# A two-layer attention encoder: rows of the input in natural order, swapped queries from DRAM, and the order of mask steps

## The chip, the core and the metric

The kernel runs on one core of one Trainium2 chip. The metric is the device time of one execution in microseconds (us). [...] VectorE is DVE, ScalarE is ACT, GpSimd is POOL; SyncE (SP) issues all DMAs.

## What is computed

Two sequences, a prompt of 1024 tokens and a sample of 512, each get 16 meta tokens in front and pass through two layers. Cut to what matters:

```
def layer(x):                                   # x: (1040 or 528) x 1024
    h = rmsnorm(x, pre_g)                       # x * rsqrt(mean(x*x) + 1e-6) * pre_g
    aq, ak, av, ag, bq, bk, bv, bg = split(h @ w_in)
    oa = window_gqa_attention(rope(aq), rope(ak), av, sink) * silu(ag)
    ob = diff_attention(rope(bq), rope(bk), bv, lam) * silu(bg)
    return x + rmsnorm(concat(oa, ob) @ w_out, post_g)
```

The windowed part has 8 query heads of 64 in 2 groups; each query sees the 16 meta tokens, the keys at a distance of at most 128, and a sink logit. The other part has 4 heads of the difference of two softmaxes over all keys. All is 32-bit.

## The kernel before, in words

**Tiling.** The 1040 + 528 = 1568 tokens lie side by side as columns, in four chunks of 392 (`CH`, L30). In layer 0 the chunks hold the tokens `ICH[0]` (L32-35): 0 to 391, 392 to 783, then 256 + 120 = 376 of them from two places, then 392. Features lie on partitions, eight blocks of 128. Each large product is made as three products of f32r halves (hi x hi, hi x lo, lo x hi), so every operand of PE is a pair of tiles.

**Order.** Every operation is first recorded with a priority; `schedule()` (L329-445) then plays a model of the engines, of the DMAs and of the buffers of each pool, and writes out one fixed order for each engine, which `emit()` (L447) issues. All instructions therefore carry line L451, and are told apart by their tiles. An engine works off its order strictly. Buffers of a pool come round in the order in which they are taken: `slot` has 16, `pp` 4 (raw weights, and much else later), `ps_t` 2 and `ps_s` 1 (both PSUM, `ps_s` of three banks), `qq` 2 (queries), `st` 1 (staged values on their way to DRAM). `START` (L50) ranks the first loads: weight 0, chunk 0, chunk 1, weight 1, the rotary table, weight 2, chunk 2, chunk 3, weight 3.

**The start of layer 0.** `load_x` (L608) brings each chunk from `xT`, the transposed input, so with features on 128 partitions: four loads for chunk 0, two for each other chunk (four for chunk 2, whose tokens come from two places). Chunk 0 is split into halves at once (L1499-1510), its scale by 1/rms is put on later. For chunks 1 to 3 `start_stats` (L1496) calls `prestats` (L723): squares on ACT or POOL, sums over the eight feature blocks on DVE, then `rstd_bc` (L693) sums over partitions with four transposes on PE, a reduce on DVE and a power on POOL, and spreads the result over all partitions with four more transposes on PE. `prenorm` (L751) then multiplies each of the eight blocks by that and by the gain, copies the high half and subtracts for the low half. The products of the first unit's four weights with the four chunks follow (`inproj`).

**The start of layer 1** is another: `pre` (L1464) takes rows that lie in natural order with tokens on partitions, already scaled, transposes four tiles of a feature block into one `ps_t` buffer, and evicts them twice: a copy with the gain (high half), and gain times value minus the high half on DVE. `stat` (L1402) makes the scale of a row: two squarings on ACT that sum along the row, one small step on DVE and one on POOL.

**Units.** Each layer then has six units: four heads of difference attention (`attn_b`) and two groups of windowed attention (`attn_a`, L1065), each overlapped with the next unit's products (`inproj`) or, at the end, with `outproj`. `attn_a` goes over the two sequences and their tiles of 128 queries, 4 heads a tile; the heads are taken in batches of three that share one `ps_s` buffer (L1145). For each tile the queries come from `AQ` in DRAM into `qt[:, 0]`; two copies from SBUF to SBUF fill `qt[:, 1]` with the two halves of the partitions swapped (L1155-1165). The three scores of a batch are followed by their mask steps, a custom instruction on DVE that adds the mask and takes the extreme of the row. One line makes the order's model hold each mask step back until the last of the three scores:

```
nc.extra = [nc.last]                       # L1176, behind the three scores
for bi, (u, i) in enumerate(batch):
```

Of the kernel before, what the change touches and what calls it, by code (L numbers as in the profile page):

```python
# [26 lines left out]
EPS = 1e-6  # L27
# [25 lines left out]
QUICK = 1  # L53
# [5 lines left out]
PRE_ACT = (0, 0, 0, 0, 0, 0, 0, 0)  # L59
# [4 lines left out]
ONLY = 4  # L64
# [478 lines left out]
def hymba_kernel(ctx, tc, xT, xr, w_in, w_out, rope, masks, pre_g, post_g, sub_g, sink_b, sink_m, lam_in, yo):  # L543
# [56 lines left out]
    def f32(ap):  # L600
        return ap.bitcast(F32)
# [6 lines left out]
    def load_x(ci):  # L608
        xin[ci] = pair()
        nc.boost = START[f"x{ci}"] * 100000  # L610
        w = 2 if ci == 0 else 4
        for k in range(0, 8, w):
            o = 0
            for t0, m in ICH[0][ci]:
                dma(xin[ci][k // 4][:, k % 4:k % 4 + w, o:o + m],
                    xT.rearrange("(a p) t -> p a t", p=128)[:, k:k + w, t0:t0 + m])
                o += m
        nc.boost = 0
# [104 lines left out]
    def prestats(xs, tmp, n, only=False):  # L723
        if only:
            for i in range(4):
                r = slice(2 * (i % 2), 2 * (i % 2) + 2)
                x, y = xs[i // 2][:, r, 0:n], tmp[i // 2][:, r, 0:n]
                nc.any((nc.scalar, "activation", (y, x, AF.Square), {}),
                       (nc.gpsimd, "tensor_tensor", (y, x, x), dict(op=ALU.mult)))
                if i:  # L730
                    nc.vector.tensor_tensor(
                        tmp[0][:, 0:2, 0:n], tmp[0][:, 0:2, 0:n], tmp[i // 2][:, r, 0:n], op=ALU.add)
            nc.vector.tensor_tensor(tmp[0][:, 0, 0:n], tmp[0][:, 0, 0:n], tmp[0][:, 1, 0:n], op=ALU.add)
        else:
            for i in range(2):
                nc.scalar.activation(tmp[i][:, :, 0:n], xs[i][:, :, 0:n], AF.Square)
            nc.any_tt(tmp[0][:, :, 0:n], tmp[0][:, :, 0:n], tmp[1][:, :, 0:n], ALU.add)
            for k in (2, 1):
                nc.any_tt(tmp[0][:, 0:k, 0:n], tmp[0][:, 0:k, 0:n], tmp[0][:, k:2 * k, 0:n], ALU.add)
        return rstd_bc(tmp[0][:, 0, 0:n], n, 1.0 / D)  # L740

    def scaled(out, x, g, rb, n, act):
        for j in range(x.shape[1]):
            if act:
                nc.scalar.activation(out[:, j, 0:n], x[:, j, 0:n], AF.Copy, scale=g[:, j:j + 1])
                nc.any_tt(out[:, j, 0:n], out[:, j, 0:n], rb[:, 0:n], ALU.mult)
            else:
                nc.vector.scalar_tensor_tensor(
                    out[:, j, 0:n], x[:, j, 0:n], g[:, j:j + 1], rb[:, 0:n], op0=ALU.mult, op1=ALU.mult)

    def prenorm(l, ci, xs, rb, n):  # L751
        his, los = [], []
        for i in range(2):
            hi, lo = pair(F32R)
            for j in range(4):
                r = slice(j, j + 1)
                h = at_p([128, 1, CN])
                scaled(h, xs[i][:, r], preg[:, l, 4 * i + j:4 * i + j + 1], rb, n, PRE_ACT[2 * ci + i])
                h = h[:, :, 0:n]
                nc.any_copy(hi[:, r, 0:n], h)  # L760
                if l == 0 and ci < QUICK:
                    nc.vector.tensor_tensor(lo[:, r, 0:n], h, f32(hi[:, r, 0:n]), op=ALU.subtract)
                else:
                    nc.any_tt(lo[:, r, 0:n], h, f32(hi[:, r, 0:n]), ALU.subtract)
            his.append(hi)
            los.append(lo)
        hT[ci] = (rows(his, 4), rows(los, 4))
# [324 lines left out]
    def attn_a(l, g):  # L1092
        S = SC[l]
        AK, AV, AQ = S["AK"][g], S["AV"][g], S["AQ"][g]
        for s in range(2):
# [502 lines left out]
```

## Time and profile before

| | |
|---|---|
| median of 3 runs | 1938.57 us (1936.39 to 1941.69) |
| the profiled execution | 1938.61 us |
| its span in the profile | 1936.8 us |
| mean granted clock of TensorE | 0.985 |
| busy: PE, DVE, ACT, POOL | 1843.4, 1515.2, 1008.1, 279.3 us |
| DMA traffic | 273.02 MB, 141 GB/s in the mean |

The span runs from the first to the last instruction of the profiled execution. Busy times are sums over instructions; an engine that is not busy stands still because something it needs is late, or because it has nothing to do. The views below give this for a stretch of the span, for a group of instructions of one form, or for single instructions in order of time.

### The profile page before, as it was taken

The page shows a single profiled execution, that of the slowest core. Times are in us where ns is not written, and L with a number is a line of the kernel's source. Part 1 is how long each engine was busy: PE and PEld are TensorE (multiplying, and loading weights), DVE is VectorE, ACT ScalarE, POOL GpSimd, SP SyncE. Part 2 cuts the span into 40 slices and gives each one's busy share as a digit, 9 for nine tenths or more (in the row PEclk, how much of TensorE's full clock was granted, in tenths as well). Part 3 has the DMA queues.
Part 4 walks back from the last instruction along what each step waited for, and adds up shares of the span by engine and source line. Part 5 has one row for each costly group of instructions (what it writes and reads, how often), then busy time and mean ns, then how long its engine had stood idle before and what let it go on. Part 6 is the DMA issues. An engine that isn't in the chain of part 4 may idle for free.

```text
span 1936.8 us, 35552 instructions
## 1 busy us (share of the span) xinstructions
PE 1843.4 (95%) x12328; PEld 1771.3 (91%) x12328; DVE 1515.2 (78%) x3363; ACT 1008.1 (52%) x2417; POOL 279.3 (14%) x516
## 2 busy tenths in 40 slices
PE   6999999999999989999789999999999999999998
PEld 5989989999989889999789999999999999889998
DVE  8858788888787787587988397787967859869767
ACT  4335445454444475575765254454545438648632
POOL 3001111211121210000221021121111101101001
PEclk8999999999999999999989999999999999999999
DMA  7253363544543657556354535445353475684464
GB/s 252 56 161 105 110 170 102 148 119 109 153 117 108 154 144 198 118 133 178 120 196 116 152 100 160 120 118 161 98 167 114 124 180 125 159 229 99 109 205 150
DMA packets 299147, 273.02 MB, mean 141 GB/s; under 512 B 101560, under 2 KB 263480, under 8 KB 298840
## 3 DMA queue, kind: packets, MB, share of 16 engines
q1 hardware_dynamic: 298968, 270.75, 50.5%
q8 instruction: 98, 1.61, 0.4%
q14 instruction: 81, 0.66, 0.1%
HBM read 149.19 MB, written 96.01 MB: 127 GB/s over the span
## 4 chain that ended last, share of the span: by engine, by line
PE 70%; DVE 11%; DMA 8%; ACT 4%; issue 4%; SPq 2%; POOL 1%; DVEq 0%; POOLq 0%; ACTq 0%
PE ps_d L451 43%; PE ps_s L451 10%; PE ps_o L451 9%; PE ps_t L451 8%; DVE at L451 2%; DVE pp L451 2%; DVE slot L451 2%; ACT pp L451 2%; SPq L451 2%; DVE sm L451 1%; DMA vv<-BV 1%; DVE og L451 1%; DMA kk<-AK 1%; DVE ru L451 1%; POOL sm L451 1%
## 5 line engine op out<-in xcount | busy, mean ns | idle before, releaser
L451 PE MATMUL ps_d<-slot,whl 128*128 128x392 f32 (+2 forms) x4560 | 938.2, 347 | 15.0 <-ACT slot L451 6.7
L451 PEld LDWEIGHTS ps_d<-slot,whl 128*128 128x128 f32 x4560 | 785.7, 190 | 22.2 <-ACT slot L451 6.7
L451 PE MATMUL ps_s<-kk,qq 128*128 128x264 f32 (+9 forms) x1496 | 284.4, 319 | 21.7 <-ACT pp L451 5.7
L451 PE MATMUL ps_o<-at,vv 128*128 128x256 f32 (+6 forms) x1368 | 285.9, 307 | 8.4 <-DVE og L451 5.5
L451 ACT ACTIVATE at<-ps_t 128x256 fp32r<-128x256 f32 (+9 forms) x434 | 187.7, 439 | 202.7 <-PE ps_t L451 177.4
L451 ACT ACTIVATE pp<-ps_s,sm 116x1040 f32<-116x1040 f32 (+4 forms) x208 | 203.9, 980 | 169.9 <-DVE sm L451 161.5
L451 DVE TENSOR_TENSOR at<-ps_t,at 128x256 fp32r<-128x256 f32 (+6 forms) x472 | 224.5, 480 | 68.0 <-ACT at L451 53.5
L451 PEld LDWEIGHTS ps_s<-kk,qq 128*128 128x128 f32 (+4 forms) x1496 | 227.2, 185 | 46.9 <-ACT pp L451 9.0
L451 PE MATMUL ps_d<-whl,slot 128*128 128x256 f32 x1800 | 259.0, 288 | 8.6 <-DVE slot L451 6.0
L451 PEld LDWEIGHTS ps_d<-whl,slot 128*128 128x128 f32 x1800 | 235.1, 192 | 14.3 <-DVE slot L451 7.2
L451 DVE TENSOR_REDUCE sm<-ps_s 116x1 f32<-116x1040 f32 (+4 forms) x208 | 218.3, 1050 | 34.3 <-PE ps_s L451 33.3
L451 ACT ACTIVATE pp<-pp,sm 128x336 f32<-128x336 f32 (+6 forms) x347 | 206.6, 607 | 61.0 <-DVE sm L451 57.6
L451 PEld LDWEIGHTS ps_o<-at,vv 128*128 128x128 f32 (+1 forms) x1368 | 214.0, 190 | 16.8 <-ACT pp L451 5.4
L451 PE MATMUL ps_t<-ident,pp 128*128 128x128 f32 (+6 forms) x1248 | 203.5, 269 | 3.1 <-DVE at L451 1.6
L451 POOL TENSOR_TENSOR pad<-pp,pad 128x64 fp32r<-128x64 f32 (+3 forms) x145 | 53.2, 370 | 819.0 <-ACT pad L451 528.1
L451 PEld LDWEIGHTS ps_t<-ident,pp 128*128 128x128 f32 (+6 forms) x1248 | 147.8, 137 | 14.7 <-ACT pp L451 2.8
L451 DVE CUSTOM_DVE_ANT_0 pp<-ps_s,mk,nsinks 128x336 f32<-128x336 f32 (+2 forms) x192 | 97.1, 528 | 22.1 <-PE ps_s L451 20.3
L451 POOL TENSOR_TENSOR sm<-sm 128x2 f32<-128x2 f32 (+3 forms) x112 | 48.7, 437 | 408.2 <-DVE sm L451 404.6
L451 POOL TENSOR_TENSOR sm<-sm,mhalf 128x1 f32<-128x1 f32 (+7 forms) x98 | 80.8, 830 | 132.9 <-DVE sm L451 129.6
L451 ACT ACTIVATE og<-ps_o 64x128 f32<-64x128 f32 (+4 forms) x248 | 66.1, 287 | 44.8 <-PE ps_o L451 27.3
L451 ACT ACTIVATE ru<-ps_d 128x392 f32<-128x392 f32 (+5 forms) x100 | 48.7, 487 | 73.9 <-PE ps_d L451 64.2
L451 DVE TENSOR_TENSOR slot<-slot 128x512 f32<-128x512 f32 (+3 forms) x79 | 73.9, 945 | 8.4 <-ACT slot L451 8.0
(158 smaller groups left out, 2130.3 us busy)
## 6 DMA issues: line engine op xcount, KB each, us to landing
wraw<-in_w_in_dram SPq DMA_DIRECT2D x46, 512.0 KB
qq<-qq SPq DMA_DIRECT2D x144, 128.0 KB
BS<-st SPq DMA_DIRECT2D x80, 196.0 KB
qq<-AQ SPq DMA_DIRECT2D x96, 128.0 KB
gl<-GT SPq DMA_DIRECT2D x72, 128.0 KB
MX<-og SPq DMA_DIRECT2D x72, 128.0 KB
slot<-MX SPq DMA_DIRECT2D x11, 768.0 KB
kk<-BS SPq DMA_DIRECT2D x8, 1040.0 KB
```

The source lines that it names most:

```text
L451: fn(*[_real(a) for a in args], **{k: _real(a) for k, a in kw.items()})
```

## The change

It has three parts.

1. Chunks 1 to 3 are loaded from `xr`, the input in natural order, a token to a partition and 4 KB to a row. Each chunk has four tiles of a quarter of its tokens (98, 94 and 98 rows; a tile whose tokens come from two places is loaded in two pieces). Chunk 1's and 2's tiles lie in `slot`, chunk 3's in the pool `p_p`. `start_stats` uses `stat` and scales the rows in place; `turned`, which is the body of `pre` made general, transposes four tiles of a feature block into one PSUM buffer and evicts them as in layer 1. Chunk 0 stays as it was. Three tuning constants and `scaled` go.
2. In `attn_a` the swapped halves of `qt[:, 1]` are loaded from `AQ` in DRAM, in place of the copies from `qt[:, 0]`.
3. The line with `nc.extra` goes, so a mask step is held back in the order's model by its own head's score alone.

The diff, cut to its core:

```diff
-QUICK = 1
-PRE_ACT = (0, 0, 0, 0, 0, 0, 0, 0)
-ONLY = 4
...
     def load_x(ci):
-        xin[ci] = pair()
+        n = sum(m for _, m in ICH[0][ci])
         nc.boost = START[f"x{ci}"] * 100000
-        w = 2 if ci == 0 else 4
-        for k in range(0, 8, w):
-            o = 0
-            for t0, m in ICH[0][ci]:
-                dma(xin[ci][k // 4][:, k % 4:k % 4 + w, o:o + m],
-                    xT.rearrange("(a p) t -> p a t", p=128)[:, k:k + w, t0:t0 + m])
-                o += m
+        if ci == 0:
+            xin[0] = pair()
+            for k in range(0, 8, 2):
+                dma(xin[0][k // 4][:, k % 4:k % 4 + 2, 0:n],
+                    xT.rearrange("(a p) t -> p a t", p=128)[:, k:k + 2, 0:n])
+        else:
+            m = n // 4
+            cols = [t0 + i for t0, k in ICH[0][ci] for i in range(k)]
+            xin[ci] = []
+            for j in range(4):
+                nc.stream = "x" if ci == 3 else "dense"
+                x = (p_p if ci == 3 else slot)([128, 2, 512])
+                a = 0
+                while a < m:
+                    t0, b = cols[m * j + a], a
+                    while b < m and cols[m * j + b] == t0 + b - a:
+                        b += 1
+                    dma(x[a:b].rearrange("p u d -> p (u d)"), xr[t0:t0 + b - a])
+                    a = b
+                nc.stream = "dense"
+                xin[ci].append(x)
...
-    def prestats(xs, tmp, n, only=False):
+    def prestats(xs, tmp, n):
...
-    def scaled(out, x, g, rb, n, act):
...
+    def stat(parts, M):
+        r = sm_p([128, 4])
+        for u, p in enumerate(parts):
+            sq = ru_p([128, 512])
+            nc.scalar.activation(sq[0:M], p, AF.Square, scale=1.0 / 32, accum_out=r[0:M, u:u + 1])
+        nc.vector.scalar_tensor_tensor(
+            r[0:M, 2:3], r[0:M, 0:1], EPS, r[0:M, 1:2], op0=ALU.add, op1=ALU.add)
+        nc.gpsimd.tensor_tensor(r[0:M, 3:4], r[0:M, 2:3], mhalf[0:M, 0:1], op=ALU.pow)
+        return r[0:M, 3:4]
...
+    def turned(l, tiles, off, n):
+        his, los = [], []
+        for u in range(2):
+            hi, lo = pair(F32R)
+            for k in range(4):
+                pt = ps_t([128, 512])
+                o = 0
+                with nc.macro():
+                    for get, M in tiles:
+                        nc.tensor.transpose(
+                            pt[:, o:o + M], get(u)[:, 128 * k:128 * k + 128], ident[0:M, 0:M])
+                        o += M
+                g = preg[:, l, 4 * u + k:4 * u + k + 1]
+                p = pt[:, off:off + n]
+                nc.any_copy(hi[:, k, 0:n], p, g)
                 nc.vector.scalar_tensor_tensor(
+                    lo[:, k, 0:n], p, g, f32(hi[:, k, 0:n]), op0=ALU.mult, op1=ALU.subtract)
             his.append(hi)
             los.append(lo)
+        return rows(his, 4), rows(los, 4)
+
+    def prenorm(ci):
+        n = sum(m for _, m in ICH[0][ci])
+        m = n // 4
+        hT[ci] = turned(0, [(lambda u, x=x: x[0:m, u], m) for x in xin[ci]], 0, n)
...
-                        if M == 80:
-                            dma(qt[:, 0, 64:80], AQ[0, :, q0:q0 + 16])
-                        for x in range(nq // qb):
-                            c = 4 * qb * x
-                            dma(qt[:, 0, c:c + 4 * qb].rearrange("p (x t) -> p x t", t=qb),
-                                AQ[:, :, q0 + qb * x:q0 + qb * x + qb].rearrange("x p t -> p x t"), 2)
-                        dma(qt[0:64, 1], qt[64:128, 0])
-                        dma(qt[64:128, 1], qt[0:64, 0])
+                        for v, d, r in ((0, 0, 0), (1, 0, 64), (1, 64, 0)):
+                            d, r = [slice(y, y + (64 if v else 128)) for y in (d, r)]
+                            if M == 80:
+                                dma(qt[d, v, 64:80], AQ[0, r, q0:q0 + 16])
+                            for x in range(nq // qb):
+                                c = 4 * qb * x
+                                dma(qt[d, v, c:c + 4 * qb].rearrange("p (x t) -> p x t", t=qb),
+                                    AQ[:, r, q0 + qb * x:q0 + qb * x + qb].rearrange("x p t -> p x t"), 2)
...
-                nc.extra = [nc.last]
                 for bi, (u, i) in enumerate(batch):
...
-            his, los = [], []
...
+            tiles = []
+            for x in range(4):
+                i = 3 * ci + x
+                M = 128 if i < 12 else 80
+                tiles.append((lambda u, i=i, M=M: xv(i // 3, u, i % 3, M), M))
+            hT[ci] = turned(l + 1, tiles, 8 * ci, CN)
...
     def start_stats(ci):
-        rb0[ci] = prestats(xin[ci], pair(), sum(m for _, m in ICH[0][ci]), ci < ONLY)
+        n = sum(m for _, m in ICH[0][ci])
+        if ci == 0:
+            rb0[0] = prestats(xin[0], pair(), n)
+        else:
+            for x in xin[ci]:
+                r = stat([x[0:n // 4, u] for u in range(2)], n // 4)
+                for u in range(2):
+                    nc.any_copy(x[0:n // 4, u], x[0:n // 4, u], r)
...
-            prenorm(0, ci, xin[ci], rb0[ci], sum(m for _, m in ICH[0][ci]))
+            prenorm(ci)
```

## Rows read from the trace of the kernel before

**Rows 1.** The page's totals: busy us (share of span) and instructions of each engine.

```profile
PE 1843.4 (95%) x12328; PEld 1771.3 (91%) x12328; DVE 1515.2 (78%) x3363; ACT 1008.1 (52%) x2417; POOL 279.3 (14%) x516
```

**Rows 2.** Stretches: length, busy PE PEld DVE ACT POOL (count), granted clock, DMA share, GB/s.

```profile
9.00:20.00 11.00, 9.52 (x36) 8.65 (x37) 11.00 (x13) 7.45 (x11) 4.42 (x2) 1.00 1.04 394
20.00:32.00 12.00, 11.92 (x70) 11.45 (x68) 11.32 (x16) 2.48 (x3) 6.26 (x4) 1.00 0.94 322
32.00:44.00 12.00, 3.88 (x18) 2.33 (x18) 9.57 (x19) 3.45 (x6) 4.94 (x3) 0.65 0.43 101
44.00:50.00 6.00, 6.00 (x20) 6.00 (x21) 6.00 (x12) 3.28 (x7) 0.00 (x0) 0.55 0.24 70
50.00:60.00 10.00, 9.71 (x57) 9.33 (x55) 5.56 (x12) 2.57 (x6) 1.42 (x2) 1.00 0.00 0
60.00:100.00 40.00, 38.72 (x226) 38.26 (x226) 34.06 (x75) 14.90 (x30) 2.32 (x4) 1.00 0.31 80
```

**Rows 3.** Order in time, DVE: start, length of one run, operation, count [idle before].

```profile
33.21 1.40 DVE L451 TENSOR_TENSOR slot<-slot 128x392 f32<-128x392 f32 x2
```

**Rows 4.** Order in time, PE, 30 to 45 us.

```profile
40.28 0.91 PE L451 MATMUL ps_t<-ident,sm 98*128 98x98 f32 x4 [5.76 <-POOL sm L451]
...
43.01 0.70 PE L451 MATMUL ps_o<-slot,whl 128*128 128x392 f32 x1
```

**Rows 5.** Stretches again: most of windowed attention in layer 0.

```profile
640.00:960.00 320.00, 298.50 (x2158) 283.32 (x2157) 252.85 (x744) 205.45 (x589) 33.84 (x65) 0.98 0.59 150
```

**Rows 6.** Groups by form: operation, count, busy us, mean ns, idle before and its releasers.

```profile
L451 ACT ACTIVATE ru<-slot 128x512 f32<-128x512 f32 x66 | 41.3, 627 | 53.3 <-DVE slot L451 51.5 <-DVE sm L451 0.7 <-DMA vv<-AV 0.6
...
L451 DVE SCALAR_TENSOR_TENSOR slot<-ps_t,preg,slot 128x392 fp32r<-128x392 f32 x32 | 19.1, 620 | 3.6 <-ACT slot L451 3.5
...
L451 ACT ACTIVATE slot<-ps_t,preg 128x392 fp32r<-128x392 f32 x22 | 12.7, 584 | 15.0 <-PE ps_t L451 15.0
```

**Rows 7.** Order in time, PE, around another group of four transposes.

```profile
76.30 0.50 PE L451 MATMUL ps_t<-ident,sm 98*128 98x98 f32 x4
76.58 0.76 PE L451 MATMUL ps_o<-slot,whl 128*128 128x376 f32 x3
```

**Rows 8.** DMA issues, 90 to 100 us, two of the stores of chunk 2's values.

```profile
BV<-st SPq DMA_DIRECT2D x1, 94.0 KB
BV<-st SPq DMA_DIRECT2D x1, 68.0 KB
```

**Rows 9.** Stretches again, one us each, while values are stored (chunk 0, chunk 2).

```profile
47.00:48.00 1.00, 1.00 (x4) 1.00 (x4) 1.00 (x3) 0.91 (x3) 0.00 (x0) 0.50 0.87 256
95.00:96.00 1.00, 1.00 (x8) 1.00 (x7) 1.00 (x3) 0.00 (x0) 0.00 (x0) 1.00 0.14 48
```

**Rows 10.** Order in time, ACT, behind the store of chunk 2's values.

```profile
99.19 0.86 ACT L451 ACTIVATE st<-ru 128x784 fp32r<-128x784 f32 x1 [5.99 <-DMA BV<-st]
```

**Rows 11.** Order in time, all engines, at 18.44 us; SPq is SP's queue of issues.

```profile
18.44 0.38 SPq L451 DMA_DIRECT2D slot<-in_x_dram  x1
18.44 1.06 ACT L451 ACTIVATE kk<-pp 128x1024 fp32r<-128x1024 f32 x1 [2.79 <-DMA pp<-in_w_in_dram]
```

**Rows 12.** Order in time, SP: two loads of a tile of queries.

```profile
703.86 0.91 SPq L451 DMA_DIRECT2D qq<-AQ  x2
```

**Rows 13.** Waits: engine, tile, releaser: us in all, how many, longest.

```profile
DVE pp L451 <- PE ps_s L451: 30.8, 19, 8.1
...
PE ps_s L451 <- DMA qq<-qq: 4.0, 5, 1.3
...
SPq L451 <- DMA qq<-AQ: 54.9, 38, 3.6
```

**Rows 14.** DMA queue, 1733 to 1737 us, only query loads: packets, MB, share of 16 engines.

```profile
q1 hardware_dynamic: 1056, 0.26, 30.9%
```

**Rows 15.** Order in time, all engines, a batch of windowed attention.

```profile
759.89 0.42 PE L451 MATMUL ps_s<-kk,qq 128*128 128x336 f32 x1 [0.57 <-DMA qq<-qq]
...
760.36 0.50 DVE L451 CUSTOM_DVE_ANT_0 pp<-ps_s,mk,nsinks 128x272 f32<-128x272 f32 x1 [2.18 <-PE ps_s L451]
```

More of the change, by code (lines that the diff above doesn't have):

```diff
@@ L721, in rows @@
         return [t[:, j] for t in tiles for j in range(k)]
-    def prestats(xs, tmp, n, only=False):
[L724 to L739, printed above, removed]
-        return rstd_bc(tmp[0][:, 0, 0:n], n, 1.0 / D)
@@ L742, in scaled @@
-    def scaled(out, x, g, rb, n, act):
[L743 to L747, printed above, removed]
-                nc.vector.scalar_tensor_tensor(
-                    out[:, j, 0:n], x[:, j, 0:n], g[:, j:j + 1], rb[:, 0:n], op0=ALU.mult, op1=ALU.mult)
-    def prenorm(l, ci, xs, rb, n):
-        his, los = [], []
[L753 to L764, printed above, removed]
+    def prestats(xs, tmp, n):
+        for i in range(4):
+            r = slice(2 * (i % 2), 2 * (i % 2) + 2)
+            x, y = xs[i // 2][:, r, 0:n], tmp[i // 2][:, r, 0:n]
+            nc.any((nc.scalar, "activation", (y, x, AF.Square), {}),
+                   (nc.gpsimd, "tensor_tensor", (y, x, x), dict(op=ALU.mult)))
+            if i:
+                nc.vector.tensor_tensor(
+                    tmp[0][:, 0:2, 0:n], tmp[0][:, 0:2, 0:n], tmp[i // 2][:, r, 0:n], op=ALU.add)
+        nc.vector.tensor_tensor(tmp[0][:, 0, 0:n], tmp[0][:, 0, 0:n], tmp[0][:, 1, 0:n], op=ALU.add)
+        return rstd_bc(tmp[0][:, 0, 0:n], n, 1.0 / D)
@@ L765, in prenorm @@
             his.append(hi)
             los.append(lo)
-        hT[ci] = (rows(his, 4), rows(los, 4))
+        return rows(his, 4), rows(los, 4)
[3 more added lines that the diff above has]
+        hT[ci] = turned(0, [(lambda u, x=x: x[0:m, u], m) for x in xin[ci]], 0, n)
     def load_w(src, pool=None, pri=0):
@@ L1400, in outproj @@
         rs = {}
-        def stat(parts, M):
-            r = sm_p([128, 4])
-            for u, p in enumerate(parts):
-                sq = ru_p([128, 512])
-                nc.scalar.activation(sq[0:M], p, AF.Square, scale=1.0 / 32, accum_out=r[0:M, u:u + 1])
-            nc.vector.scalar_tensor_tensor(
-                r[0:M, 2:3], r[0:M, 0:1], EPS, r[0:M, 1:2], op0=ALU.add, op1=ALU.add)
-            nc.gpsimd.tensor_tensor(r[0:M, 3:4], r[0:M, 2:3], mhalf[0:M, 0:1], op=ALU.pow)
-            return r[0:M, 3:4]
         def norm(ci, j, M):
@@ L1466, in pre @@
                 return
-            his, los = [], []
-            for u in range(2):
-                hi, lo = pair(F32R)
-                for k in range(4):
-                    d = slice(128 * k, 128 * k + 128)
-                    pt = ps_t([128, 512])
-                    with nc.macro():
-                        for x in range(4):
-                            i = 3 * ci + x
-                            M = 128 if i < 12 else 80
-                            h = xv(i // 3, u, i % 3, M)[:, d]
-                            nc.tensor.transpose(pt[:, 128 * x:128 * x + M], h, ident[0:M, 0:M])
-                    g = preg[:, l + 1, 4 * u + k:4 * u + k + 1]
-                    p = pt[:, 8 * ci:8 * ci + CN]
-                    nc.any_copy(hi[:, k], p, g)
-                    nc.vector.scalar_tensor_tensor(lo[:, k], p, g, f32(hi[:, k]), op0=ALU.mult, op1=ALU.subtract)
-                his.append(hi)
-                los.append(lo)
-            hT[ci] = (rows(his, 4), rows(los, 4))
+            tiles = []
[4 more added lines that the diff above has]
+            hT[ci] = turned(l + 1, tiles, 8 * ci, CN)
         steps = dict(b=first, s=second, S=lambda *c: second(*c, keep=False), f=fetch, p=post, n=pre, l=load, g=gains)
```

## The prediction

> **What bounds the kernel now.** I read the page's totals first, then the table of stretches over the start, then the order of instructions on DVE and PE in the one stretch where PE is poorly used, and last the waits and stretches of the two places in each layer where windowed attention runs. TensorE is busy for 95% of the span, the next engine, DVE, for 78% [rows 1]: whatever keeps PE from working costs its full length, and time on another engine costs nothing until PE waits for it.
>
> The start is the exception. From 50 to 60 us PE runs 57 matmuls in 9.71 busy us at full granted clock, 0.170 us each; from 32 to 50 it runs 18 + 20 = 38, which at that pace is 6.5 us of work [rows 2]. [...] The cause is a chain on DVE and POOL: chunk 1's squares are still being summed at 33.2 us, behind chunk 0's evictions [rows 3], the column sums on PE, a reduce on DVE and the power on POOL follow, and PE's broadcast, which waits 5.76 us for that power, comes at 40.28, the first product of chunk 1 at 43.0 [rows 4].
>
> In the stretch of windowed attention in layer 0 PE is busy 298.5 of 320 us [rows 5], so 21.5 us are open there; the one of layer 1 is alike.
>
> **The change, part by part.** All is counted against the profiled execution, 1938.6 us (span 1936.8 and 1.8 around it); the median of the runs shown is the same 1938.6.
>
> *Statistics and transposes.* Per chunk from 1 to 3, four squarings, four sums, the reduce, the power and broadcast, and eight times scale, copy and subtract go. In come eight ACT squarings of 512 at 0.627 us, four small DVE and POOL steps, eight row scalings, and eight evictions of a transposed group: a copy at 0.58 on ACT and a subtract at 0.62 on DVE [rows 6]. DVE gives up eight scalings, eight subtracts, the adds (1.40 for two of them [rows 3]) and the reduce, and takes eight subtracts at 0.62 and four small steps: the eight scalings, some 5 us a chunk, are what it saves. ACT takes 8 x 0.627 = 5.0 more, and part of the row scalings. Both have room: DVE's 11.3 of 12 us before 32 is what the change relieves, and ACT has 2.5 of 12 there [rows 2]. The long chain of rows 3 and 4 is gone: chunk 1's statistics can be done soon after its rows land near 15 us. If nothing else is late, the 11.5 us come back.
>
> PE pays for it: 24 groups of four transposes come in and 6 go. A group with the same shape (98 partitions, 98 columns) pushes the next matmul from 76.30 to 76.58 us, so 0.3 us [rows 7], and 18 x 0.3 = **+5.4 us**, which no work hides.
>
> *The load of chunk 2.* Here I expect the change to lose what it gains. Chunk 2 holds 376 tokens, four tiles of 94 rows, of which one is split into 68 and 26. No load of before has such a row count, but the stores of chunk 2's values have exactly these, at 1 KB a row: 94 and 68 KB [rows 8]. While the 94-row pieces go out, the 16 DMA engines are busy for 0.14 of the time and move 48 GB/s; around the store of chunk 0's 98-row tiles they reach 0.87 and 256 GB/s [rows 9], and the loads of now, on 128 partitions, 394 GB/s [rows 2]. ACT waits 6.0 us for such a store to land [rows 10]. 0.14 is close to 2 of 16, 0.87 to 14 of 16: a transfer seems to spread only as far as its row count divides. [...]
>
> The price: a 94-row tile is 385 KB, at 48 GB/s 8.0 us, three of them 24 us; the 68-row piece lies between nothing and 5.8 us, I take 3. Against 1.54 MB at 394 GB/s, 3.9 us, if the load spreads well. I take 27, because the nearest row has the same row count. It starts near 20 us: SP issues a DMA when the one eight places before has landed (the 19th, chunk 2's first, goes at 18.44, in the moment in which w2, the 11th, has landed and ACT starts on it) [rows 11], and the bytes ahead are nearly the same. So chunk 2 is whole near 47 us, and with the last tile's squarings (two, 1.3), power, scaling and first group, some 5 us in all, its products start near 52.
>
> What covers that? Chunks 0 and 1 with three weights. The fourth (w3) sits behind chunk 3 in pool pp, whose four buffers go to w0 to w2 and chunk 3's tiles, and it can load only when those are transposed. That is 144 matmuls, 24.5 us, and eight groups, 2.4 us. From 9 us with the 4.9 us that PE loses before 20 already [rows 2], PE runs dry near 41. It idles 11 us, and resumes at half clock as it does now (44 to 50: 20 matmuls where 35 fit, 2.6 us lost). So 13.6 us are lost in place of 11.5. The start comes to -11.5 + 13.6 + 5.4 = **+7.5 us**; bounds -6.1 (the load in time) and +13.5. The upper end adds 6 us: ACT and DVE work in order, and chunk 2's squarings, or an eviction that waits for a store queued on the same few engines, can hold up chunk 1's copies too, as the 6.0 us wait of rows 10 shows.
>
> *Swapped queries from DRAM.* Two dependent copies per tile become four loads that wait for nothing; with 52 tiles (two head groups of 12 in either layer, 4 small ones) that is 104 issues more on SP, at 0.91 / 2 = 0.46 us [rows 12] 48 us. SP loses 54.9 us of waiting for the first loads, which pays for them, and PE waits for the swap 4.0 us in all [rows 13]. Such loads moved 0.26 MB in 1056 packets with all engines busy for 0.309 x 4 us = 1.24 us, 0.21 MB a us [rows 14]; the copies that go moved as many bytes. I take **-2 us**, bounds -4.0 and +2. [...]
>
> *Masks.* The edit frees only the written order. The trace says that the wait is real and on the whole buffer: the batch's last score, 336 columns wide, ends at 760.31, and its first mask, of another head with 272 columns, starts only then, at 760.36, with DVE idle for 2.18 us [rows 15]. If PE's later score in the same buffer now comes behind a mask in the order, it would wait for that mask, 0.50 us and 0.05 us on either side of it, 0.6 us, with all of PE's queue behind it. There are 196 heads in 68 batches. DVE's idle time before masks, 30.8 us [rows 13], is the most it could gain, but PE seldom waits for it. Bounds: -2, and +11 if a quarter of the batches stalls once (17 x 0.6 = 10); DVE, nearly always busy there, usually reaches a mask after the third score is issued, so I take **+2**.
>
> Sum: 1938.6 + 7.5 - 2 + 2 = **1946** (slower by 0.4%). Its own range is 1941 to 1953.
>
> **The rivals.** *Chunk 2's load is in time* (it spreads over the engines, or the copies of chunk 1 and w3 cover it): -11.5 + 5.4 - 2 = -8, **1930.5**. For it speaks that the loads of now fill the engines; against it the stores with the same row counts. *The change doesn't show*: the swap and masks win 4 to 6 us more in the windowed stretches' open time, or relief on DVE pays at 60 to 100 us, and **1939** results. Against it: PE is already 38.7 of 40 us busy there [rows 2]. *Masks stall PE*: as forecast at the start, but the +11 in place of +2, **1955**. It decides from 10 batches on (10 x 0.6 = 6 us). For it: the wait on the whole buffer; against: scores of one batch mostly come back to back.
>
> **How the numbers follow.** 0.3% is 5.8 us, about what a measurement of this kernel can tell from no change. Forecast 0.56 (slower by more than 0.3% 0.42, within 0.14), load in time 0.20 (faster 0.17, within 0.03), no change 0.10 (within 0.09, faster 0.01), masks stall 0.14 (slower). Faster 0.18, same 0.26, slower 0.56. Range 1929 to 1958: it takes in the fast rival and most of the stalled one, and leaves about 1 in 10 on each side.
>
> **What would show it.** Right: a stretch of some 20 us, from 20 us on, with DMA share near 0.14 and 48 GB/s; ACT idle until chunk 2's tiles land; PE idle near 40 to 52 us with the granted clock at 0.5 after it. Wrong: DMA share near 0.9 until 33 us, then silence, and PE without a gap; or, in the windowed stretches, PE waits for DVE's mask step that exceed 5 us in sum. If PE's lost time at the start is the same 11 us and the total still falls, the windowed stretches carry the change and my small terms were the wrong ones.

## The result, and the profile after

The changed kernel takes 2006.43 us in the median of 4 runs (1998.82 to 2009.66), the kernel before 1937.48 us in the runs beside it: the ratio is 1.0349, with an interval of 1.0312 to 1.0385. 1946 was forecast, in a range of 1929 to 1958. The change makes the kernel slower, as forecast, but by 69 us where 7 were expected. The profiled execution of the changed kernel was the fastest of its runs, 1998.8 us with a span of 1997.0, so its trace shows 60 of the 69 us.

The totals of the page, as in [rows 1]:

```profile
PE 1867.3 (94%) x12400; PEld 1788.3 (90%) x12400; DVE 1487.5 (74%) x3315; ACT 1039.5 (52%) x2492; POOL 276.9 (14%) x525
```

PE (TensorE) is idle for 129.7 us in place of 93.4, and busy for 24 us more, of which the 72 added transposes explain some 5 (18 groups at 0.28 us). In the trace 58 us of PE's work lie in stretches with the granted clock (TensorE's, as a share of full speed) at 0.5, before 38. Three products of 392 columns take 0.98 us there (from 46.82 us on) and 0.54 at 1.00 (from 50.55 on); at that pace the 20 us more are some 9 of the 24, an estimate from these two. The other 10 stay open. DVE has lost 28 us of work and ACT has gained 31, as the change says.

**The start.** The stretches that answer to [rows 2], then three of two us each (stretch, length, busy PE, PEld, DVE, ACT, POOL with counts, granted clock, DMA share, GB/s):

```profile
9.00:20.00 11.00, 7.28 (x29) 6.62 (x30) 8.98 (x14) 8.49 (x22) 0.00 (x0) 0.94 1.00 304
20.00:32.00 12.00, 11.60 (x69) 11.05 (x68) 8.43 (x19) 6.79 (x12) 3.25 (x6) 0.91 0.55 172
32.00:44.00 12.00, 1.99 (x10) 1.67 (x9) 2.75 (x7) 4.43 (x12) 0.54 (x1) 0.66 0.47 138
44.00:60.00 16.00, 10.33 (x51) 9.69 (x49) 6.16 (x25) 8.69 (x23) 1.62 (x3) 0.71 0.33 95
60.00:100.00 40.00, 38.24 (x240) 37.63 (x241) 30.05 (x61) 20.14 (x36) 3.26 (x6) 0.92 0.29 77
38.00:40.00 2.00, 0.00 (x0) 0.00 (x0) 0.00 (x0) 0.00 (x0) 0.00 (x0) 0.50 0.12 49
52.00:54.00 2.00, 2.00 (x14) 1.99 (x12) 0.00 (x0) 0.24 (x1) 0.00 (x0) 1.00 0.13 53
58.00:60.00 2.00, 0.00 (x0) 0.00 (x0) 0.00 (x0) 1.38 (x5) 0.00 (x0) 0.50 0.09 17
```

The 94-row loads do what the stores of [rows 9] did: a DMA share of 0.12 to 0.13 and 49 to 53 GB/s, with no engine of the core at work from 38 to 40 us. PE has two gaps, each with the clock at 0.5 from inside the gap until 5 to 6 us behind it (from 35.8 to 49.5 and from 56.3 to 66.5 us). Order in time of the changed kernel, all engines (start, length, operation, count, idle before and its releaser), at the two gaps:

```profile
9.32 2.12 SPq L448 DMA_DIRECT2D pp<-in_xr_dram  x2
...
21.45 9.30 SPq L448 DMA_DIRECT2D slot<-in_xr_dram  x5
...
32.27 9.04 SPq L448 DMA_DIRECT2D pp<-in_xr_dram  x2
...
34.26 0.63 ACT L448 ACTIVATE ru<-slot 94x512 f32<-94x512 f32 x1 [5.20 <-DMA slot<-in_xr_dram]
...
41.41 16.05 SPq L448 DMA_DIRECT2D BS<-st  x8
41.76 0.63 ACT L448 ACTIVATE ru<-slot 94x512 f32<-94x512 f32 x1 [5.28 <-DMA slot<-in_xr_dram]
...
42.51 0.57 DVE L448 TENSOR_TENSOR ru<-ps_o,rb 128x392 f32<-128x392 f32 x1 [5.03 <-ACT ru L448]
...
43.13 1.35 PE L448 MATMUL ps_o<-slot,whl 128*128 128x392 f32 x3 [10.01 <-DVE ru L448]
...
45.98 0.63 ACT L448 ACTIVATE ru<-slot 94x512 f32<-94x512 f32 x1 [1.34 <-DMA slot<-in_xr_dram]
...
53.76 0.63 ACT L448 ACTIVATE ru<-slot 94x512 f32<-94x512 f32 x1 [5.35 <-DMA slot<-in_xr_dram]
...
60.39 0.69 DVE L448 CAST st<-ps_t 98x512 fp32r<-98x512 f32 x1 [4.18 <-DMA BS<-st]
61.00 0.62 DVE L448 SCALAR_TENSOR_TENSOR slot<-ps_t,preg,slot 128x392 fp32r<-128x392 f32 x1
...
61.76 0.89 PE L448 MATMUL ps_t<-ident,slot 98*128 98x98 f32 x4 [7.43 <-DVE slot L448]
```

Read the first gap from its end. PE waits 10.0 us for DVE's eviction `ru<-ps_o`; DVE waits 5.0 us for ACT, whose squarings of chunk 2 write their unused squares into the same two `ru` buffers; and ACT waits 5.3 us for a tile of chunk 2. The four tiles are released at 34.26, 41.76, 45.98 and 53.76, that is 7.5, 4.2 and 7.8 us apart: one after the other. The second gap is the stores': SP spends 9.0 us on two loads and 16.1 us on eight stores of chunk 0's results, waits included; the one staging buffer `st` is not free until they land, DVE's next use of it waits until 60.39, and the subtract for a block of chunk 1 that PE needs stands behind it, at 61.00. SP's longest wait among the stores (50 to 58 us) is for the last 94-row tile:

```profile
SPq L448 <- DMA slot<-in_xr_dram: 5.7, 1, 5.7
```

**The windowed stretches.** The waits of PE, as in [rows 13]:

```profile
PE ps_s L448 <- DVE sm L448: 15.6, 31, 1.0
PE ps_s L448 <- DMA qq<-AQ: 11.0, 7, 3.2
```

Before, the first of these had 1.9 us in 3 waits. `sm` is the row extreme that a mask step writes: 31 scores wait for a mask step. Two of them in the order of time:

```profile
706.18 0.57 DVE L448 CUSTOM_DVE_ANT_0 pp<-ps_s,mk,nsinks 128x336 f32<-128x336 f32 x1
...
706.68 0.08 DVE L448 DVE_READ_ACCUMULATOR2_ANT sm<- 128x1 f32 x1
...
706.81 0.89 PE L448 MATMUL ps_s<-kk,qq 128*128 128x336 f32 x4 [0.56 <-DVE sm L448]
...
708.00 0.57 DVE L448 CUSTOM_DVE_ANT_0 pp<-ps_s,mk,nsinks 128x336 f32<-128x336 f32 x1
708.50 0.08 DVE L448 DVE_READ_ACCUMULATOR2_ANT sm<- 128x1 f32 x1
...
708.63 0.58 PE L448 MATMUL ps_s<-kk,qq 128*128 128x336 f32 x2 [0.93 <-DVE sm L448]
```

In both, PE starts 0.05 us after the mask step's second instruction has ended. They are not of one kind. Counted through in the trace, the score at 706.81 is the first of the next batch, which has to wait for the one buffer anyway; all 3 waits of before are of this kind. The score at 708.63 is the third of a batch and waits for the mask step of the first: it goes to another third of the buffer than the one that is read (`sp[0:M, bi]` with another `bi`). Of the 31 waits, 23 with 11.2 us are of this second kind, 8 with 4.3 us of the first.

**Where the time is lost.** A way to compare kernels whose orders differ: give each matmul the lower quartile of the start-to-start times of its form in the traces of before and after, leave the transposes out, and note when the sum of finished work passes a mark. The table has that time for the kernel before, and for the others how much later (+) or earlier they pass it. The marks up to 311 lie in the start and the first units of layer 0. The mask steps of layer 0 begin at 652 us in the kernel before, so 583 lies early in its windowed part; 583 to 778 span the rest of it and the output products behind it, 1283 to 1556 the windowed part and the output products of layer 1. Each line is one execution, the profiled one; most lie within 6 us of the median of their kernel, but that of the changed kernel 8 and that of e1 9 us below it, and that of e13 13 us above.

```
product work done, us    39    117    311    583    739    778   1283   1361   1556
before, at             70.0  158.7  389.1  733.2  926.4  999.3 1590.5 1689.2 1928.4
after                 +19.0  +21.6  +21.1  +22.1  +50.7  +26.5  +39.8  +56.7  +61.1
e1  start only        +18.2  +21.0  +22.2  +16.4  +20.2  +21.1  +22.2  +23.0  +19.8
e2  queries only       +0.1   -0.0   +0.2   -2.6  +11.3   -7.4   +4.8   +7.2   +7.7
e3  masks only         -0.6   -0.7   +1.1   -2.6  +15.5   -1.6  +11.1  +16.0  +22.1
e4  after, rows of 16  -1.2   +2.0   +3.8   +3.3  +31.5   +7.9  +19.8  +37.8  +39.5
e5  start, rows of 16  -0.3   +1.7   +4.6   +4.5  +10.2  +11.0  +13.9  +14.4   +9.4
e6  e5, weight 1 first -3.4   -2.7   +4.3   +6.9  +16.6   +5.2  +14.0  +17.5  +14.7
e7  start, told        +21.9  +23.3  +29.6  +31.3  +40.8  +27.5  +37.3  +38.9  +35.6
e8  masks, known       -1.5   -2.0   -1.4   +4.0   +3.3   -1.3   +8.4  +10.5  +14.0
e9  before, jitter a   +1.7   +2.3   +8.2   +0.9  +12.1  +13.5  +39.5  +38.0  +30.5
e10 before, jitter b   -1.5   -0.0   +3.7   -1.5  +13.8  +14.7  +15.9  +16.0  +15.7
e11 after, two repairs -2.7   +1.7   +6.5  +15.5  +30.8  +14.1  +21.3  +21.3  +20.9
e12 e6, jitter a       -2.5   -6.2   -5.0   +1.7  +13.3   +2.7  +10.7  +10.6   +4.0
e13 masks, jitter a    +0.0   -0.1   +5.3   -0.3  +17.0  +11.2  +34.6  +52.7  +66.3
e14 masks, jitter b    -0.2   +0.6   +3.3   +0.8  +12.7   +3.2   +3.9  +15.0  +17.1
e15 queries, jitter a  +2.4   +3.0   +8.5   +2.9  +20.5  +16.9  +34.0  +37.4  +33.9
e16 e6, other jitter   -2.4   -0.7   +5.7  +12.8  +19.6  +12.9  +14.5  +14.4  +11.9
```

The changed kernel loses 20 us at the start and never gets them back, 28.6 in the windowed part of layer 0, of which 24 come back, 13 between the windowed parts, where the change touches nothing, and 21 in the windowed part of layer 1. That last stretch, before and then in the changed kernel, with the wait that costs PE most in it:

```profile
1590.50:1928.40 337.90, 325.55 (x2349) 310.60 (x2347) 265.96 (x723) 198.61 (x570) 35.27 (x58) 0.98 0.56 154
1630.30:1989.50 359.20, 332.95 (x2348) 314.71 (x2346) 266.13 (x706) 201.07 (x569) 34.33 (x63) 0.98 0.54 147
PE ps_s L448 <- DVE sm L448: 5.8, 10, 1.0
```

PE's idle time grows by 13.9 us and its busy time by 7.4. Only 5.8 us of that are waits for a mask step, where before had none.

### The profile page after: what moved, and what is told of

Same layout as the page of the kernel before. It is cut to its first block, busy times and chain, and to the rows that moved or that the text cites. A ratio compares the mean times of both kernels' runs of the same rounds, so it can differ in the third digit from the quotient of the medians.

```text
span 1997.0 us, 35918 instructions
## 1 busy us (share of the span) xinstructions
PE 1867.3 (94%) x12400; PEld 1788.3 (90%) x12400; DVE 1487.5 (74%) x3315; ACT 1039.5 (52%) x2492; POOL 276.9 (14%) x525
## 5 line engine op out<-in xcount | busy, mean ns | idle before, releaser
L448 PE MATMUL ps_s<-kk,qq 128*128 128x264 f32 (+9 forms) x1496 | 293.9, 323 | 45.2 <-DVE sm L448 15.6
L448 ACT ACTIVATE at<-ps_t 128x256 fp32r<-128x256 f32 (+10 forms) x439 | 190.4, 439 | 187.0 <-PE ps_t L448 162.5
L448 ACT ACTIVATE pp<-pp,sm 128x336 f32<-128x336 f32 (+7 forms) x356 | 213.1, 611 | 105.4 <-DVE sm L448 91.4
L448 PEld LDWEIGHTS ps_d<-whl,slot 128*128 128x128 f32 x1800 | 234.2, 190 | 13.5 <-DVE slot L448 8.8
L448 PE MATMUL ps_t<-ident,pp 128*128 128x128 f32 (+6 forms) x1280 | 211.6, 271 | 2.3 <-DVE pp L448 1.8
L448 PEld LDWEIGHTS ps_t<-ident,pp 128*128 128x128 f32 (+6 forms) x1280 | 153.0, 138 | 14.3 <-issue 2.1
L448 POOL TENSOR_TENSOR sm<-sm 128x2 f32<-128x2 f32 (+2 forms) x112 | 49.2, 440 | 502.9 <-DVE sm L448 456.2
L448 POOL TENSOR_TENSOR sm<-sm,mhalf 128x1 f32<-128x1 f32 (+6 forms) x107 | 83.9, 790 | 205.8 <-DVE sm L448 195.9
L448 ACT ACTIVATE ru<-slot 128x512 f32<-128x512 f32 (+2 forms) x82 | 51.3, 626 | 75.3 <-DVE slot L448 57.0
L448 ACT ACTIVATE og<-ps_o 64x128 f32<-64x128 f32 (+4 forms) x248 | 66.5, 287 | 45.4 <-DVE og L448 21.2
L448 ACT ACTIVATE ru<-ps_d 128x392 f32<-128x392 f32 (+5 forms) x94 | 45.7, 486 | 82.0 <-PE ps_d L448 66.5
```

Source lines behind the costliest of these rows:

```text
L448: fn(*[_real(a) for a in args], **{k: _real(a) for k, a in kw.items()})
```

## The experiments

**The parts alone.** e1 is the changed kernel with both edits of `attn_a` taken back; e2 and e3 are the kernel before with one of them.

```diff
# e1: queries by copies, nc.extra kept
-                        for v, d, r in ((0, 0, 0), (1, 0, 64), (1, 64, 0)):
...
+                        dma(qt[0:64, 1], qt[64:128, 0])
+                        dma(qt[64:128, 1], qt[0:64, 0])
...
+                nc.extra = [nc.last]
# e2: the loop over v, d, r in place of the copies
# e3:
-                nc.extra = [nc.last]
```

> Only the first part of the change: chunks 1 to 3 in natural order, transposed by PE; queries and mask order as before. Theory (the three parts each cost on their own and nearly add): in the trace of the changed kernel the same amount of product work is done 23 us later at 115 us than before, so this kernel is about 23 us slower, 1955 to 1967. Rival (the whole written order has been shuffled and the sum is an accident of it): a time that is not near +23, above all one within 5 us of before or over +40.

> Only the second part: the swapped query halves loaded from DRAM. Theory: PE's scores wait 11.0 us for such loads in the changed kernel, against 4.0 us for the copies before, both in all; so +5 to +15 us. Rival (the loads are free and the masks alone cost the windowed stretches): within 4 us of before. The prediction had -2.

> Only the third part: each mask step waits in the order's model for its own head's score. Theory: scores wait behind masks (31 waits, 15.6 us in the changed kernel), so +10 to +20 us, with a row of waits of PE scores for DVE's mask step near 15 us. Rival (the loads of the queries pull the scores apart, and masks alone cost nothing): within 5 us of before, with that row near the few us that it has before.

e1: 1967.46 us, ratio 1.0162 (1.0126 to 1.0197), so +31; its profiled execution, the fastest of its runs at 1958.4, has 20 of them, all of them lost by the first two marks. e2: 1941.54, ratio 1.0027 (1.0011 to 1.0043), +5. e3: 1960.30, ratio 1.0124 (1.0099 to 1.0149), +24. The sum is 60 of 69 us, so the parts come near to adding. For e1 and e3 the theory holds so far, though e1 ends at the edge of the time that was expected and e3 above the +10 to +20. e2 lies at the lower end of what the theory expected, but its rival's row is the one that is seen: PE waits 1.6 us for the query loads in it, less than for the copies before.

**Rows of 16.** e4 is the changed kernel, and e5 is e1, with chunk 2 cut into tiles of 96, 96, 96 and 88 rows; the loads then have 96, 64 + 32, 80 + 8 rows.

```diff
+    def xrows(ci):
+        n = sum(m for _, m in ICH[0][ci])
+        return (96, 96, 96, 88) if n == 376 else (n // 4,) * 4
...
+                    if b - a == 88:
+                        b -= 8
                     dma(x[a:b].rearrange("p u d -> p (u d)"), xr[t0:t0 + b - a])
```

> The whole change, but chunk 2's four tiles have 96, 96, 96 and 88 rows in place of 94 each (the third comes in 64 and 32 rows, the last in 80 and 8). Theory (the 94-row loads run on 2 of 16 DMA engines and hold up ACT's and SP's queues behind them): the stretch at 0.13 DMA share from 36 us on is gone, PE has no gap of 10 us there, and 15 to 25 us of the 69 come back: 1981 to 1991. Rival (chunk 2 is late for another reason, such as SP's queue or the buffers): the gaps stay, and the time stays within 6 us of the changed kernel's 2006.

> The first part alone, with chunk 2's tiles of 96, 96, 96 and 88 rows as in the run before; queries and masks as in the kernel before. Theory (parts add): first part alone was +30, rows of 16 gave back 24, so within 8 us of before, 1932 to 1946, with PE without a gap of 5 us until 60 us. Rival (what the start wins is lost later to an order made for other times): 1950 or more.

e4: 1982.15 us, ratio 1.0247 (1.0210 to 1.0285): 24 of the 69 us are back, inside what the theory expected. e5: 1951.67, ratio 1.0080 (1.0055 to 1.0105): 16 us better than e1, but outside the 1932 to 1946 that were expected and inside the rival's range: by the table it loses 10 us between the marks 583 and 1361. In e4, the stretch in which chunk 2 comes in, the squaring of its last tile, for which ACT has no wait, and two stretches that stood still in the changed kernel:

```profile
26.00:34.00 8.00, 7.60 (x50) 7.05 (x50) 8.00 (x17) 7.97 (x18) 1.32 (x1) 1.00 1.04 233
37.04 0.62 ACT L448 ACTIVATE ru<-slot 88x512 f32<-88x512 f32 x1
36.00:38.00 2.00, 2.00 (x14) 1.96 (x14) 1.93 (x10) 2.00 (x6) 0.13 (x1) 1.00 1.00 283
38.00:40.00 2.00, 2.00 (x14) 1.78 (x14) 1.97 (x8) 1.92 (x6) 0.68 (x2) 1.00 0.95 300
```

All 16 DMA engines are at work, with 233 GB/s while chunk 2 comes in and 283 to 300 GB/s later, for chunk 3 and the stores. The last tile is squared at 37.04 in place of 53.76, PE is busy, and both gaps are gone. With the loads in time the start stands at -0.3 (e5) and -1.2 us (e4) where the first part alone stood at +18.2. The row count of a load is what cost the start its 20 us.

**Weight 1 ahead of chunk 1.** e6 is e5 with two ranks exchanged.

```diff
-START = {'w0': 9, 'x0': 8, 'x1': 7, 'w1': 6, ...
+START = {'w0': 9, 'x0': 8, 'x1': 6, 'w1': 7, ...
```

> As the run with rows of 16 and the first part alone, but weight 1 is loaded ahead of chunk 1. In the changed kernel PE waits from 15.2 to 18.7 us for that weight, which lies behind chunk 1's four loads. Theory: this wait goes and the time falls by 2 to 5 us against the same kernel without it. Rival (chunk 1's rows are then late by the same time): no difference above 2 us.

1947.64 us, ratio 1.0055 (1.0032 to 1.0077); 4 us below e5, as the theory expected, with intervals that overlap. The table shows the same at its first mark: -3.4 where e5 has -0.3. In e5 PE stands still for 3.55 us up to 19.54, right behind DVE's wait for weight 1, which the four loads of chunk 1 had kept waiting; in e6 it works through from 9 to 17.5 us.

**The order told how slow the loads are.** e7 is e1 with the model's cost of the 94- and 68-row loads raised; the loads stay.

```diff
-                    dma(x[a:b].rearrange("p u d -> p (u d)"), xr[t0:t0 + b - a])
+                    dma(x[a:b].rearrange("p u d -> p (u d)"), xr[t0:t0 + b - a],
+                        6 if b - a == 94 else 3 if b - a == 68 else 1)
```

> The first part alone with chunk 2 in 94 rows, but the model that makes the order is told that a load of 94 rows takes 6 times and one of 68 rows 3 times as long as its bytes say. The loads themselves are unchanged. Theory (most of the loss is ACT's and DVE's order, which has chunk 2's squarings ahead of chunk 1's evictions, and not the load itself): ACT no longer stands at 28 to 34 us, PE's first gap goes or moves to after 40 us, and 8 to 20 of the 30 us come back. Rival (the loads are the loss and no order hides them): within 6 us of the first part alone.

1974.42 us, ratio 1.0185 (1.0152 to 1.0218): 7 us more than e1, against the theory, and a little outside the rival's 6. Its stretches, and the end of its gap in order of time:

```profile
32.00:44.00 12.00, 12.00 (x83) 11.62 (x82) 10.69 (x38) 7.02 (x17) 2.40 (x3) 1.00 0.36 118
50.00:60.00 10.00, 0.56 (x4) 0.30 (x4) 2.10 (x7) 5.33 (x13) 1.61 (x3) 0.74 0.16 52
60.00:70.00 10.00, 0.00 (x0) 0.00 (x0) 2.70 (x6) 2.40 (x5) 0.54 (x1) 0.50 0.34 80
```

```profile
68.75 0.60 ACT L448 ACTIVATE st<-ps_t 98x512 fp32r<-98x512 f32 x1 [6.01 <-DMA BS<-st]
69.38 0.69 DVE L448 TENSOR_TENSOR st<-ps_t,st 98x512 fp32r<-98x512 f32 x1 [5.63 <-ACT st L448]
...
70.13 0.89 PE L448 MATMUL ps_t<-ident,slot 94*128 94x94 f32 x4 [19.57 <-DVE st L448]
```

The first gap is gone (PE is busy for 12.00 of 12 us where the changed kernel had 1.99), so ACT's order had made it. But chunk 2's last tile still comes at 54.4 us, the stores still go out behind it, and one gap of 19.6 us takes the place of two. This order moved the loss and did not lessen it; others were not tried.

**Masks with the wait known.** e8 is the kernel before with each later score of a batch recorded behind the mask step of the one ahead, as the buffer demands wherever a mask step comes first (the 23 waits of the second kind).

```diff
+                    nc.extra = [sm_done] if bi else []
                     with nc.macro():
                       for v in range(2):
                         nc.tensor.matmul(
...
-                nc.extra = [nc.last]
-                for bi, (u, i) in enumerate(batch):
...
+                    sm_done = nc.last
```

> The kernel before, with each later score of a batch made to wait, in the order's model too, for the mask step of the score ahead of it: the wait on the shared PSUM buffer is then in all 128 places, but known. Theory (the masks' loss is a wait that the model does not know, so it puts the score right behind the mask; where it knows, it puts other products between): PE's waits for DVE's mask step fall below 8 us in sum and the time lies within 8 us of before. Rival (each such wait costs its 0.6 us wherever it is): 128 x 0.6 = 77 us, so 1990 or more.

1948.04 us, ratio 1.0065 (1.0038 to 1.0092). The row of waits, of e3 first and then of e8:

```profile
PE ps_s L451 <- DVE sm L451: 17.8, 26, 2.3
```

```profile
PE ps_s L451 <- DVE sm L451: 2.9, 5, 1.2
```

128 known waits cost PE 2.9 us, 26 unknown ones 17.8. The rival's 77 us are out. The time is 10 us above before, 2 more than the theory allowed; by the table most of it is lost between the marks 778 and 1283, where the edit does nothing.

**Only the order.** e9 and e10 are the kernel before with a random addend below 4 places on each priority.

```diff
-SPREAD = 0
+SPREAD = 4
# e10 also: SEED = 37 in place of 36
```

> The kernel before, nothing changed but the order: each operation's priority gets a random addend below 4 places, so neighbours in the recorded order may change places. A measure of how much an accident of the order is worth. Theory (the three parts cost by their own mechanisms): within 4 us of before, so that the queries' +4 and the leftover +10 to +14 of the repaired kernels are effects. Rival (any new order is several us slower than this one): +4 to +20 us, and then the small differences say nothing of their parts.

> As the run before it, with another seed. Theory: within 4 us of before. Rival: +4 to +20 us, and different from the other seed by some us.

e9: 1969.35 us, ratio 1.0162 (1.0142 to 1.0182), +32. e10: 1948.64, ratio 1.0068 (1.0049 to 1.0087), +11. The rival is right in both, and in e9 by more than it said: a kernel in which nothing is changed but which neighbour goes first loses 11 or 32 us. In e9 most of it lies between the marks 778 and 1283, in layer 1's first units, which no part of the change touches. Any difference of 10 us between two of these kernels is therefore no evidence for a mechanism unless a row of waits or the table shows it in its place.

**Both repairs.** e11 is e4 with the edit of e8.

> The whole change with both repairs: chunk 2 in rows of 96, 96, 96 and 88, and each later score's wait for the mask ahead of it known to the model. Theory (parts add): the changed kernel is +69; rows of 16 give back 24, known waits give back 12, so 1967 to 1976. Rival (the two losses hide each other in part): 1977 or more; if most of what is left is an accident of the order, 1950 to 1966.

1955.60 us, ratio 1.0091 (1.0074 to 1.0108): 51 of the 69 us are back, more than the 36 of the two repairs alone. That is below the 1967 to 1976 of the theory that parts add, and in the range that was named for an accident of the order.

**The pairs.** e12 is e6 with the seed of e9, e16 is e6 with an addend below 2 and seed 40; e13 and e14 are e3 with the addends of e9 and e10; e15 is e2 with the seed of e9. The addends are drawn one by one as operations are recorded. The mask edit records no more operations than before, so e13 and e9, and e14 and e10, are strict pairs; the queries' edit and the first part record more, so from there on e15 and e12 have other addends than e9.

> The first part with rows of 16 and weight 1 ahead of chunk 1 (1947.6 as it stood, with its start 3.4 us ahead of before at the same amount of work and 16 us behind by 540 us), with the same random addend below 4 places. Theory (what it loses behind the start is an accident of the order): the time moves by more than 4 us, either way, and may fall to 1935 to 1943. Rival (it belongs to the transposes and the new loads): 1944 to 1951.

> The mask part alone, on the order jittered with the first seed; its pair without the mask part had 1969.4 us, with 0.4 us of PE waiting for DVE's mask step. Theory (waits of scores behind masks in the shared buffer, some 15 us, come with the edit in any order): that row is 10 us or more, and the time is 8 to 25 us above the pair. Rival (the edit's cost was an accident of the order): the row stays below 5 us, or the time is within 6 us of the pair or below it.

> The mask part alone, on the order jittered with the second seed; its pair had 1948.6 us, with 2.7 us of PE waiting for DVE's mask step. Theory: the row is 10 us or more and the time 8 to 25 us above the pair. Rival: below 5 us, or the time within 6 us of the pair or below it.

> The queries' part alone, with the first seed's jitter (pair 1969.4 us, where PE's scores wait 6.0 us for the copies). Theory (the loads cost some 5 us by themselves): 1972 to 1980, with waits for query loads above 6 us. Rival (the loads cost nothing that shows, the +4 was an accident of the order): anything outside 1972 to 1980, with waits for query loads below 4 us.

> The first part with rows of 16 and weight 1 ahead of chunk 1, with a random addend below 2 places and another seed. Theory (its start is worth some 5 us, and what comes behind is an accident of the order): ahead of the kernel before by 2 to 8 us at the work done by 300 us, and a time anywhere from 1930 to 1960. Rival (what it loses behind belongs to the transposes): 1944 to 1951 again.

e12: 1946.37 us (1.0050, interval 1.0034 to 1.0066), 1 us from e6 and in the rival's range. e13: 1991.64 (1.0292, 1.0247 to 1.0338), 22 above its pair e9. e14: 1954.79 (1.0093, 1.0058 to 1.0129), 6 above its pair e10. e15: 1967.91 (1.0152, 1.0111 to 1.0192), 1.4 below e9. e16: 1951.85 (1.0075, 1.0052 to 1.0098), a time that the theory allowed, but without the lead that it expected by 300 us. The mask row of e9, e13, e10 and e14, in this order:

```profile
PE ps_s L451 <- DVE sm L451: 0.4, 1, 0.4
```

```profile
PE ps_s L451 <- DVE sm L451: 14.5, 25, 2.0
```

```profile
PE ps_s L451 <- DVE sm L451: 2.7, 3, 2.1
```

```profile
PE ps_s L451 <- DVE sm L451: 13.3, 26, 0.7
```

In three orders (e3, e13, e14) the mask edit brings 25 or 26 waits and 13 to 18 us; the same orders without it have 1 to 3. Counted through as above, 24 of the 26 of e3 are later scores of a batch, of which the kernel before has none. The table says what the edit is worth in layer 1: from the mark 1283 to 1556 the five kernels with the edit and the wait unknown (after, e3, e4, e13, e14) lose 11 to 32 us, the other twelve between -9 and +6. The waits for mask steps are 6 to 10 us of that in each of the five, most of it in e3 and e14. In the other three more than half lies in PE's other waits and in longer busy time; two of these have the other edits too, and what makes that half is not shown. In layer 0 the two groups overlap, and most of it comes back with the output products. The time of e14 alone, 6 us above its pair, would not have shown it. A buffer for each score in place of one for three, which would take the wait away, was not tried. e15 speaks for the queries' rival: no loss against e9, and 2.0 us of PE's waits for the loads where e9 has 6.0 for the copies. e12 and e16 bracket the repaired first part: e12 is 2 to 6 us ahead of before up to the mark 311, e16 is 6 behind there, and neither ends ahead of the kernel before. No version tried beats it.

## Why the prediction was wrong, point by point

- **What bounds the start** was read rightly (the 11.5 us of the sum are the 18 us from 32 to 50 less their 6.5 us of work [rows 2]), and the fate of the chain in [rows 3, 4] too: with the loads in time it is gone. A group of transposes costs what was said: one pushes the next matmul from 49.64 to 49.92 us in the changed kernel, 0.28 against the 0.3 used.
- **The load of chunk 2**: the mechanism, few of the 16 engines for 94 rows, is shown by the share of 0.12 to 0.13, by e4 with its 1.04, and by the marks of completion that a DMA leaves in the trace. In the changed kernel a 94-row load leaves 2 behind the one of its issue, a 98-row load 14, the pieces of 68 and 26 rows leave 4 and 13, and a load of 128 rows leaves 16. That a mark stands for an engine is an estimate from these counts and the share: 2 of 16 is 0.125. The 3 us taken for the 68-row piece are shown by no run by themselves; the tile of 68 and 26 rows was released 4.2 us behind the one before it. The length was right: from one tile's 7.5 us ahead of the first release, at 34.26, to the last at 53.76 it is 27 us. The start was not. "It starts near 20 us" is the step that failed: it took the moment of issue for the start. Other loads were still ahead of it when SP issued it: already before, the one issued at 18.44 [rows 11] was whole only at 26.15, by its marks of completion in the trace, and ACT began on chunk 2 at 27.09 (the line below). "The bytes ahead are nearly the same" holds: 7258 KB are issued ahead of chunk 2 before and 7018 KB in the changed kernel, with chunk 3's first two tiles (9.32) among them and two loads of weights fewer. But they move more slowly, from 9 to 20 us with 304 GB/s in place of 394. Chunk 2's first load is issued at 21.45, and counted back from its release it ran from 26.8. So chunk 2 was whole at 53.7 and not at 47.

```profile
27.09 0.83 ACT L451 ACTIVATE slot<-slot 128x752 f32<-128x752 f32 x1 [6.28 <-DMA slot<-in_x_dram]
```

- **What waits for it** is the term that was mis-sized most at the start. "PE runs dry near 41" supposed that PE would have chunks 0 and 1 to itself until then. It ran dry at 33, since chunk 2's squarings hold ACT and the two `ru` buffers that DVE's evictions need, and again at 54, since chunk 0's stores hold `st`. The prediction named both ("can hold up chunk 1's copies too") and priced them together at 6 us, as an upper end. They cost 10.0 and 7.4, each with a stretch at half clock. So the start lost 19 to 22 us at equal work where +7.5 was the sum and +13.5 the bound. e7 adds that an order made for slow loads did not save it.
- **The fast rival** was right in its price and not in its reach: -6.1 us at the start is what e12 shows (-6.2 at the mark 117), though that it fits so well is luck: e6 and e16 have -2.7 and -0.7 there. And e5 with the loads in time has only -0.3 at the first mark, because weight 1 came late.
- **Queries**: the reason for the -2 us holds alone (e2, e15: fewer waits than the copies had). The -2 itself is not shown: e2 is 4 to 5 us slower than before, e15 1.4 us faster than e9, both less than a new order does. In the changed kernel the loads do make PE wait 11.0 us, in e4 6.1, in e11, where the masks' waits are known, 2.8. The changed kernel and e4 have the same row of mask waits, so these alone do not set it; what does is open.
- **Masks**: the mechanism was named, with its price of 0.6 us a wait (15.6 us over 31 waits is 0.5). The step that failed is "DVE, nearly always busy there, usually reaches a mask after the third score is issued": a scheduler that does not know of the wait puts the score where the mask is running. At 31 waits the same price gives +16 to +19, above the bound of +11. And the price is only a part: e3 is 24 us slower with 17.8 us of such waits, and in layer 1 of the changed kernel they are 5.8 of the 21 us.
- **The missing term.** Nothing in the sum stood for the new order itself. e9 and e10 show +32 and +11 for that alone; 13 us of the changed kernel's loss lie where the change does nothing. Which of its instructions would have to move is not settled.
- The range failed because its upper end added the masks' rival to the forecast start, where both had errors of the same sign, and had no room for the order.

## What to carry to other kernels

When loads are re-cut, look at the row counts before the bytes: four tiles of 94 rows took 27 us, at 49 to 53 GB/s where nothing else moved; in rows of 96, 96, 96 and 88 the same chunk came in while all 16 engines moved 233 GB/s. A scheduler's model has to know every wait that the hardware program will really have: in e3 26 unknown waits cost PE 18 us, in e8 128 known ones 3. And measure what a mere reshuffle of the order costs before a small difference is put down to an edit.

## What was not expected of the hardware

The loads on few DMA engines did not only come late, one by one (7.5, 4.2 and 7.8 us apart). While they were on their way, SP needed 16.05 us for eight stores of other data, 5.7 of them in the one wait for the last 94-row tile; in the run with rows of 16 (e4) the same eight took

```profile
33.13 6.08 SPq L448 DMA_DIRECT2D BS<-st  x8
```

Transfers that do spread, with 16 marks, are held up as well. The first 94-row load, issued at 21.45, has two behind the one of its issue, at 33.48 and 34.17. The load of a later weight (`wraw`), issued at 30.79 behind the 94-row loads, leaves 16: 14 by 35.96, the last two at 54.38 and 54.93, right behind the last 94-row tile at 53.67. The last of the eight stores, issued at 57.15, has 14 by 58.54 and the last two at 59.59 and 60.12; DVE's use of `st` follows at 60.39. In e4 `wraw`, issued at 27.50, is whole at 36.01. The two late marks fit two DMA engines that still have the 94-row loads to work off; which engine a mark belongs to, the trace does not tell. A slow load is paid for by what SP issues behind it, too.
